# First stage of a hybrid mLSTM and attention layer: who issues the loads of x, and where two small gate copies run

## The chip, the cores and the metric

The kernel runs on one core of one Trainium2 chip. The metric is the device time of one execution in microseconds (us). Three executions of the kernel before gave 3497.74, 3498.3 and 3503.58 us; their median is 3498.3 us. All inputs, outputs and intermediate tensors are in 32-bit floating point.

## The reference, cut to what matters

```python
def encoder_layer(x, ...):                      # two groups of tokens: 2048 and 256, 1024 features
    h = rmsnorm(x, norm1_w)
    p = h @ w_in                                # 1024 -> 2848 columns
    mq, mk, mv, mo, gates, aq, ak, av = split(p)
    m_out = mlstm_mixer(mq, mk, mv, mo, gates, ...)   # 8 heads, both directions, output gate mo
    a_out = attention_mixer(aq, ak, av, ...)          # 8 query heads, 2 key heads, normed q and k, rotary
    x = x + concat([m_out, a_out]) @ w_out
    h = rmsnorm(x, norm2_w)
    a, g = split(dwconv3(h @ w_up))
    return x + (silu(g) * a) @ w_down           # then a final rmsnorm
```

The `gates` are 32 columns per token: input and forget gates of 8 heads in two directions. The forget gates go through a log-sigmoid, and running sums and maxima of the gates over the tokens give the stabiliser m, which every mLSTM chunk uses.

## The kernel before, in words

The 2304 tokens are cut into 18 tiles of 128. The work has four stages: the first stage (`phase_a`, with `gate_math` behind it), attention and mLSTM woven into each other, the output projection, and the feed-forward part. Each engine runs its instructions in the order of its own list. A scheduler puts those lists together from the order in which the program emits its operations and from its own estimate of their times, so an edit in one place can shift neighbours in another. A helper, `issue_after`, lets the program say that some instruction comes behind a given one in that list.

The first stage goes through the tiles in a fixed order, tiles 16 and 17 first and then 0 to 15. In this document "tile n" is the n-th in that order, from 0 to 17. For each tile:

- `front_a` (L167) loads x (512 KB), squares it on ScalarE (ACT, L173), and adds the eight pieces in three steps on GpSimd (POOL, L179 and L180). `rstd_bc` sums over the features with a small matmul (L127), adds epsilon on VectorE (DVE, L130), raises to the power -1/2 on POOL (L131), and spreads the result with another small matmul (L133).
- `front_b` (L183) multiplies x with it on DVE (L187), makes a rounded copy on ACT (L188) and the rest on DVE (L189), and stores both, 1 MB, to `n_d` from the queue of SyncE (SP, L190). Once DVE is through, the buffer of x is free. There are three such buffers beside the two that tiles 0 and 1 use.
- `mm` (L222) does the 48 matmuls of the tile for attention's columns and the gates (L232).
- `post_a` and `post_b` evict on ACT (L241, L243), sum squares (DVE, L251), raise to the power on POOL (L96, L97), apply norm and rotary on DVE (L257 to L275, with one rounding on ACT, L274), and store q to `q_d` from the SP queue (L276).
- `post2` transposes k on PE (L310), evicts on ACT (L311) and stores it from the ACT queue.
- `gates` (L279) works on groups of two or four tiles: log-sigmoid on DVE and ACT, then for each tile a copy that spreads the gates over 64 columns (`gp`, L299, DVE), two transposes on PE (L303), and an eviction of 40 x 256 elements into `rows` (L304, DVE).

The loop interleaves these: while tile n is multiplied, `front_b` of tile n+3 and `front_a` of tile n+4 run. The load of x is inside `front_a`, so it is emitted four tiles ahead, and it is issued from the SP queue, which also carries the stores to `n_d` and `q_d` and the loads of the mLSTM weights (L103).

Once the last tile is multiplied, `gate_math` scans `rows` (L372, L374), makes the stabiliser and its derived tables, and stores `nm_d` (L454); PE meanwhile begins the mLSTM projections (L688, L698), whose PSUM buffer is single.

In the mLSTM, `out_a` (L783) prepares a chunk: a load of m (`dm`, from `nm_d`, L785) and, for every second chunk of the first three head pairs, a load of the output gate (`ogr`, from `og_d`, L797), both issued from the POOL queue. The loads of attention's keys and values (L489 to L492) are issued from POOL too.

Of the kernel before, what the change touches and what calls it, by code (L numbers as in the profile page):

```python
# [9 lines left out]
F32 = mybir.dt.float32  # L10
F32R = mybir.dt.float32r
AF = mybir.ActivationFunctionType
# [5 lines left out]
P = 128  # L18
D = 1024
NCC = D // P  # L20
T1, T2 = 2048, 256
T = T1 + T2
NT = T // P
# [18 lines left out]
NX0 = 2  # L42
# [42 lines left out]
def f32(ap):  # L85
    return ap.bitcast(F32)
# [50 lines left out]
def phase_a(g, tc, sw, st_x, after_x, after_mm, after_pj, wm):  # L137


    nc = g.nc  # L140
    with ExitStack() as st:
# [9 lines left out]
        sx = st_x.enter_context(tc.tile_pool(name="a_x", bufs=2, side="right", reuse_waits="tile"))  # L151
# [8 lines left out]
        order = list(range(NT1, NT)) + list(range(NT1))  # L160

        first = [sw.tile([P, D], F32, tag="w", name=f"first{k}", bufs=WB) for k in range(8)]
        xw = [first[k].rearrange("p (c t) -> p c t", c=NCC) for k in range(NX0)]

        xs = {}

        def front_a(i):  # L167

            n = order.index(i)
            x = xw[n] if n < NX0 else sx.tile([P, NCC, P], F32, tag="x", name=f"x{i}", bufs=3)  # L170
            nc.sync.dma_start(x, g.xT[i])
            xq = sx.tile([P, NCC, P], F32, tag="xq", name=f"xq{i}", bufs=2)
            nc.scalar.activation(xq, x, AF.Square, scale=1.0 / 32.0)  # L173
            sq = sf.tile([P, P], F32, tag="sq", name=f"sq{i}")
            if n == 0:
                nc.vector.tensor_reduce(sq, xq.rearrange("p c t -> p t c"), AX.X, ALU.add)
            else:
                for k in (4, 2):
                    nc.gpsimd.tensor_tensor(xq[:, 0:k], xq[:, 0:k], xq[:, k:2 * k], ALU.add)  # L179
                nc.gpsimd.tensor_tensor(sq, xq[:, 0], xq[:, 1], ALU.add)  # L180
            xs[i] = x, rstd_bc(g, sf, pp if n else pj_, [sq], P, "rs" if n else "pj", f"a{i}", bufs=2)
# [11 lines left out]
        def weights(cs):  # L193
            for c in cs:
                r = first[NX0 + c] if NX0 + c < 8 else sx.tile([P, D], F32, tag="x", name=f"ra{c}", bufs=3)
                split(g, ws[c][:, 0, :], ws[c][:, 1, :], g.w_a[c], r[:, 0:800], g.n1w[:, c:c + 1])

        def tables():
            nc.sync.dma_start(bgb, g.b_gates.to_broadcast([P, 32]))
            for n in (slice(0, 4), slice(4, NT1)):  # L200
                nc.sync.dma_start(tab[:, n, 0], g.rope.rearrange("(n p) a d -> p n a d", p=P)[:, n])
            nc.sync.dma_start(qkw[:, 0, :], g.q_norm_w.to_broadcast([P, HD]))
            nc.sync.dma_start(qkw[:, 1, :], g.k_norm_w.to_broadcast([P, HD]))
            for t in gps:
                nc.gpsimd.memset(t, 0.0)
            for a in range(2):
                for r in range(2):
                    for h in range(2):
                        o, s = r * 32 + h * 16, r * 32 + (1 - h) * 16
                        nc.vector.tensor_copy(rot[:, a, o:o + 16], qkw[:, a, s:s + 16])  # L210
            for t in (qkw, rot):
                nc.vector.tensor_scalar(t[:, 0, :], t[:, 0, :], 0.125, None, ALU.mult)


        def tables2(n):
            eng = nc.gpsimd if n.start else nc.vector
            for a in (1, 0):
                for r, t in enumerate((qkw, rot)):
                    eng.tensor_tensor(tab[:, n, a, r, :], tab[:, n, 0, r, :],
                                            t[:, a:a + 1, :].to_broadcast([P, n.stop - n.start, HD]), ALU.mult)  # L220
# [58 lines left out]
        def gates(i0, n):  # L279

            f = g.gtm[:, i0:i0 + n, 1, :]
            t4 = sp.tile([P, 4, 4, 16], F32, tag="t4", name=f"t4_{i0}", bufs=1)
            na, u, ln, dl = (t4[:, k, 0:n] for k in range(4))
            nc.vector.scalar_tensor_tensor(na, f, -1.0, f, ALU.mult, ALU.min)
            nc.scalar.activation(na, na, AF.Exp)
            yield
            nc.vector.tensor_scalar(u, na, 1.0, None, ALU.add)
            nc.vector.scalar_tensor_tensor(dl, u, 1.0, na, ALU.subtract, ALU.subtract)
            nc.scalar.activation(ln, u, AF.Ln)
            nc.vector.tensor_scalar(u, u, -0.5, 1.5, ALU.mult, ALU.add)  # L290
            nc.vector.tensor_tensor(dl, dl, u, ALU.mult)
            yield
            nc.vector.tensor_tensor(ln, ln, dl, ALU.subtract)
            nc.vector.scalar_tensor_tensor(f, f, 0.0, ln, ALU.min, ALU.subtract)
            for i in range(i0, i0 + n):
                if i % 2 == 0:
                    yield
                gp = gps[i % 3]
                nc.vector.tensor_copy(gp.rearrange("p a (b z) -> p a b z", b=2)[:, :, :, 0:8],  # L299
                                      g.gtm[:, i].rearrange("p a (b h) -> p a b h", b=2))  # L300
                pg = pp.tile([40, 2, P], F32, tag="pk", name=f"pg{i}")
                for a in range(2):
                    nc.tensor.transpose(pg[:, a, :], gp[:, a, 0:40], g.ident)  # L303
                nc.vector.tensor_copy(g.rows[:, :, i * P:(i + 1) * P], pg)  # L304

        def post2(i, kz):
            pk = pp.tile([P, 2, P], F32R, tag="pk", name=f"pk{i}")
# [3 lines left out]
            nc.scalar.activation(kT, f32(pk), AF.Copy)  # L311
            nc.scalar.dma_start(g.k_d[:, :, i * P:(i + 1) * P].rearrange("g p t -> p g t"), f32(kT))

        front_a(order[0])
        front_b(order[0])
        weights(range(0, 3))
        front_a(order[1])
        front_b(order[1])
        weights(range(3, 6))
        front_a(order[2])  # L320
        front_b(order[2])
        weights(range(6, NCC))
        tables()
        tables2(slice(0, 2))
        front_a(order[3])
        prev = None
        steps = []
        for n, i in enumerate(order):
            pj, = mm(i)
            if n:  # L330
                post2(order[n - 1], prev)
            if n == NT - 1:
                st_f.close()
                after_mm()
            qk, r = post_a(i, pj)
            with ExitStack() as behind:
                if n + 3 < NT:
                    behind.enter_context(tc.issue_after(front_b(order[n + 3]).ins))
                    if n + 4 == NT:
                        st_x.close()  # L340
                        after_x()
                prev = post_b(i, qk, r)
                if steps:
                    for _ in range(2 if n == NT - 1 else 1):
                        next(steps[0], None)
                if n < 7:
                    tables2(slice(2 * n + 2, min(2 * n + 4, NT1)))
                if wm:
                    wm.pop(0)()
            if n + 4 < NT:  # L350
                front_a(order[n + 4])
            if n == NT - 1:
                st_j.close()
                after_pj()
            if n % 4 == 1:
                for _ in (steps.pop() if steps else ()):
                    pass
                steps = [gates(*((NT1, 2) if n == 1 else (i - 3, 4)))]
                next(steps[0])
# [284 lines left out]
def mlstm(g, tc, s1, sp, sw, sn, pj_, pm):  # L644


    nc = g.nc
# [133 lines left out]
    def out_a(s, i):  # L781
        nm = f"{s.p}_{i}"
        o = Pair()  # L783
        o.dm = sp.tile([P, 2, 2, P], F32, tag="dm", name="dm" + nm, bufs=DMB)
        nc.gpsimd.dma_start(o.dm.rearrange("p d h l -> p (d h l)"),  # L785
                          g.nm_d[i, 4 * s.p:4 * s.p + 4].rearrange("r l -> (r l)").unsqueeze(0).to_broadcast([P, 4 * P]))
        for d in range(2):
            sgn = 1 - 2 * d
            nc.gpsimd.affine_select(out=o.dm[:, d], in_=o.dm[:, d], compare_op=ALU.is_ge, fill=NEG, base=0,
                                    pattern=[[0, 2], [sgn, P]], channel_multiplier=-sgn)  # L790
            for h in range(2):
                nc.scalar.activation(o.dm[:, d, h], o.dm[:, d, h], AF.Exp,
                                     bias=tm[:, i, 0, d, 2 * s.p + h:2 * s.p + h + 1])
        if s.p < LASTP:
            if i % 2 == 0:
                s.og = s1.tile([P, 2, P], F32, tag="ogT", name="ogr" + nm, bufs=OTB)
                nc.gpsimd.dma_start(s.og, g.og_d[s.p, i // 2])  # L797
            o.og = s.og[:, i % 2]
        return o

# [87 lines left out]
    s = weights(0)  # L888
    yield from proj_steps(s)
    for p in range(4):  # L890
# [3 lines left out]
        if p < 3:  # L894
# [4 lines left out]
            while True:  # L899
                a, b = next(outs, None), next(ps, None)  # L900
# [3 lines left out]
            s = s2  # L904
# [558 lines left out]
```

## Time and profile before

| what | value |
|---|---|
| median of the runs | 3498.3 us (3497.74 to 3503.58) |
| the profiled execution, its own time | 3496.09 us |
| its span in the trace | 3494.4 us |
| TensorE (PE) busy | 3401.6 us |
| VectorE (DVE) busy | 2346.9 us |
| ScalarE (ACT) busy | 1680.2 us |
| GpSimd (POOL) busy | 1101.4 us |
| HBM read and written | 315.55 MB and 82.72 MB |

PE is busy nearly all the time, so the places to read are its idle stretches, what ended each of them, and the granted clock, which is the share of full speed at which PE may run. In a list of instructions each row has the start and the duration in us, the engine, the line of the kernel, the operation, what it writes and reads, and in brackets how long the engine sat idle before and what released it. "SPq" and "POOLq" are the queues of those engines. In a list of waits each row names who waited, for whom, the total in us, how often, and the longest. The first stage lasts from the start to about 212 us, the gates' tail behind it to about 250 us.

### The profile page before, as it was taken

The page shows a single profiled execution, that of the slowest core. Times are in us where ns is not written, and L with a number is a line of the kernel's source. Part 1 is how long each engine was busy: PE and PEld are TensorE (multiplying, and loading weights), DVE is VectorE, ACT ScalarE, POOL GpSimd, SP SyncE. Part 2 cuts the span into 40 slices and gives each one's busy share as a digit, 9 for nine tenths or more (in the row PEclk, how much of TensorE's full clock was granted, in tenths as well). Part 3 has the DMA queues.
Part 4 walks back from the last instruction along what each step waited for, and adds up shares of the span by engine and source line. Part 5 has one row for each costly group of instructions (what it writes and reads, how often), then busy time and mean ns, then how long its engine had stood idle before and what let it go on. Part 6 is the DMA issues. An engine that isn't in the chain of part 4 may idle for free. (4 is left out here: it accounts for less than half of the span.)

```text
span 3494.4 us, 53250 instructions
## 1 busy us (share of the span) xinstructions
PE 3401.6 (97%) x19538; PEld 3027.3 (87%) x19538; DVE 2346.9 (67%) x4008; ACT 1680.2 (48%) x3809; POOL 1101.4 (32%) x1298
## 2 busy tenths in 40 slices
PE   7999999999999999999999999999999999999998
PEld 6788777777777777767788999998999999999998
DVE  6874364546544555664445888878888878887777
ACT  4544354444444454453333544445544445555555
POOL 6752022213231321311125333225433224422222
PEclk9999999999999999999999999999999999999999
DMA  6764233233243434442247332213423213312221
GB/s 218 244 196 135 81 119 96 83 119 95 89 128 111 136 112 136 130 138 79 86 157 249 120 105 96 73 69 122 143 98 103 73 67 124 140 63 70 73 68 54
DMA packets 252629, 401.76 MB, mean 115 GB/s; under 512 B 27984, under 2 KB 152688, under 8 KB 252368
## 3 DMA queue, kind: packets, MB, share of 16 engines
q1 hardware_dynamic: 220272, 355.87, 30.5%
q0 software_dynamic: 10640, 31.86, 3.1%
q10 hardware_dynamic: 21456, 10.62, 1.0%
q8 instruction: 154, 2.52, 0.3%
q14 instruction: 107, 0.88, 0.1%
HBM read 315.55 MB, written 82.72 MB: 114 GB/s over the span
## 5 line engine op out<-in xcount | busy, mean ns | idle before, releaser
L1203 PE MATMUL pd<-act,wd 128*128 128x384 f32 (+1 forms) x3120 | 591.2, 335 | 17.0 <-DVE acc L1205 11.3
L1203 PEld LDWEIGHTS pd<-act,wd 128*128 128x128 f32 x3120 | 539.5, 188 | 24.0 <-DVE acc L1205 14.7
L581 PE MATMUL pv<-pe,vv 128*128 128x512 f32 x1040 | 514.5, 593 | 0.2
L547 DVE TENSOR_REDUCE mx<-px 128x1 f32<-128x512 f32 (+1 forms) x528 | 342.5, 673 | 194.2 <-PE px L546 192.5
L1065 PE MATMUL pa<-nt,wut 128*128 128x386 f32 (+2 forms) x2376 | 455.0, 339 | 1.5 <-ACT u L1081 1.5
L1065 PEld LDWEIGHTS pa<-nt,wut 128*128 128x128 f32 x2376 | 422.2, 190 | 1.8 <-ACT u L1081 1.8
L571 ACT ACTIVATE pe<-ps 128x512 f32<-128x512 f32 x520 | 292.5, 595 | 262.2 <-PE ps L570 258.6
L1159 DVE SCALAR_TENSOR_TENSOR y<-u,cw,y 128x768 f32<-128x768 f32 (+1 forms) x264 | 307.9, 1167 | 36.0 <-ACT y L1152 29.0
L1070 POOL TENSOR_TENSOR tw<-ru 128x512 f32<-128x512 f32 x66 | 96.4, 1461 | 744.5 <-DMA ru<-w_up 536.5
L1205 DVE TENSOR_TENSOR acc<-pd,acc 128x384 f32<-128x384 f32 (+1 forms) x544 | 281.4, 538 | 37.5 <-PE pd L1203 36.5
L1081 ACT ACTIVATE u<-pa 128x386 f32<-128x386 f32 (+2 forms) x264 | 128.8, 488 | 327.1 <-PE pa L1065 325.0
L581 PEld LDWEIGHTS pv<-pe,vv 128*128 128x128 f32 x1040 | 189.0, 189 | 82.5 <-issue 57.8
L569 PE MATMUL ps<-qq,kk 128*128 128x512 f32 x520 | 249.8, 483 | 0.1
L949 PE MATMUL po<-cmx,wo 128*128 128x256 f32 x1728 | 241.7, 290 | 1.6 <-DVE wo L106 1.6
L949 PEld LDWEIGHTS po<-cmx,wo 128*128 128x128 f32 x1728 | 220.8, 190 | 25.4 <-issue 17.8
L546 PE MATMUL px<-kk,qq 128*128 128x512 f32 (+1 forms) x528 | 224.4, 455 | 2.6 <-ACT pe L571 1.7
L688 PE MATMUL mj<-mn,wm 128*128 128x256 f32 x1296 | 212.2, 303 | 5.8 <-ACT og L702 4.5
L688 PEld LDWEIGHTS mj<-mn,wm 128*128 128x128 f32 x1296 | 180.7, 193 | 34.7 <-issue 20.6
L570 PE MATMUL ps<-qm,kl 65*128 65x512 f32 x520 | 207.4, 402 | 0.0
L698 PE MATMUL mv<-wm,mn 128*128 128x256 f32 x1296 | 206.3, 298 | 0.9 <-ACT qb L694 0.9
L698 PEld LDWEIGHTS mv<-wm,mn 128*128 128x128 f32 x1296 | 178.4, 192 | 22.3 <-issue 14.2
L232 PE MATMUL pj<-w_a,n1T 128*128 128x512 f32 (+1 forms) x864 | 178.9, 362 | 5.7 <-ACT n1T L188 4.5
(283 smaller groups left out, 6629.8 us busy)
## 6 DMA issues: line engine op xcount, KB each, us to landing
ru<-w_up SPq DMA_DIRECT2D x132, 512.0 KB, 3.2
mn<-n_d SPq DMA_DIRECT2D x216, 256.0 KB, 3.3
rd<-w_down SPq DMA_DIRECT2D x66, 512.0 KB, 3.3
n_d<-n1T SPq DMA_DIRECT2D x18, 1024.0 KB, 5.6
dm<-nm_d POOLq DMA_DIRECT2D x72, 256.0 KB, 3.6
mjn<-n_d SPq DMA_DIRECT2D x72, 256.0 KB, 3.0
mvn<-n_d SPq DMA_DIRECT2D x72, 256.0 KB, 3.2
q_d<-qz SPq DMA_DIRECT2D x18, 512.0 KB, 3.1
```

The costliest lines, as they stand in the source:

```text
L546: nc.tensor.matmul(ps[:, 0:w], s.qq[:, t * P:(t + 1) * P], s.kv[z0][0][:, 0:w], start=True, stop=True)
L547: nc.vector.tensor_reduce(s.mx[:, t, z0:z0 + 1], ps[:, 0:w], AX.X, ALU.max)
L569: nc.tensor.matmul(ps[:, 0:N], kk[:, kc:kc + P], s.qq[:, 0:N], start=True, stop=False)
L571: nc.scalar.activation(pe[:, z, 0:N], ps[:, 0:N], AF.Exp)
L581: nc.tensor.matmul(s.pv[:, 0:N], s.kv[kp // 2][2][:, kt % 4, :], pe[:, z, 0:N], start=(kt == 0), stop=(kt == s.nk - 1))
L688: nc.tensor.matmul(pj[:, o], s.w[c][:, a, o * P:(o + 1) * P], nT[c][:, :, h, :], start=(c + o + k == 0), stop=(c == NCC - 1 and k == 2 and ...
L698: nc.tensor.matmul(pv[:, o], nT[c][:, o, a, :], s.w[c][:, h, 256:512], start=(c + o + k == 0), stop=(c == NCC - 1 and k == 2 and o == 1))
L949: nc.tensor.matmul(po[:, o], wo[c][z // 2][:, a, n], mx[c][:, h, :], start=(c == 0 and k == 0), stop=(c == NCC - 1 and k == 2))
L1065: nc.tensor.matmul(p, w[:, aa, c, :], ops[k][:, c, bb, 0:n], start=c == 0 and i == 0 and not add, stop=c == NCC // 2 - 1 and i == 2, skip_ ...
L1159: nc.vector.scalar_tensor_tensor(y[:, s:e], u[:, s + k:e + k], cw[:, k, jj:jj + 1], y[:, s:e], ALU.mult, ALU.add)
L1203: nc.tensor.matmul(po, wds[j][c // 4][:, aa, c % 4 * P:(c % 4 + 1) * P], acts[j][:, bb, z0:z1], start=(j == 0 and k == 0), stop=(j == len( ...
L1205: nc.vector.tensor_tensor(accs[c][:, z0:z1], po, accs[c][:, z0:z1], ALU.add)
```

## The change

The load of x leaves `front_a` and becomes `load_x`. The first four tiles' loads still go out from SP; the other 14 go out from POOL. In the loop they are emitted for tile n+5, just ahead of `front_a` of tile n+4. The number of buffers stays three. The copy `gp` goes from DVE to POOL, the eviction into `rows` from DVE to ACT. The load of the output gate must stand behind the chunk's load of m in POOL's list. Nothing else in the program text changes.

```diff
+        def load_x(i):
+            n = order.index(i)
+            xs[i] = x = xw[n] if n < NX0 else sx.tile([P, NCC, P], F32, tag="x", name=f"x{i}", bufs=3)
+            (nc.sync if n < 4 else nc.gpsimd).dma_start(x, g.xT[i])
+
         def front_a(i):
 
             n = order.index(i)
-            x = xw[n] if n < NX0 else sx.tile([P, NCC, P], F32, tag="x", name=f"x{i}", bufs=3)
-            nc.sync.dma_start(x, g.xT[i])
+            x = xs[i]
...
-                nc.vector.tensor_copy(gp.rearrange("p a (b z) -> p a b z", b=2)[:, :, :, 0:8],
+                nc.gpsimd.tensor_copy(gp.rearrange("p a (b z) -> p a b z", b=2)[:, :, :, 0:8],
                                       g.gtm[:, i].rearrange("p a (b h) -> p a b h", b=2))
...
-                nc.vector.tensor_copy(g.rows[:, :, i * P:(i + 1) * P], pg)
+                nc.scalar.activation(g.rows[:, :, i * P:(i + 1) * P], pg, AF.Copy)
...
+        load_x(order[0])
         front_a(order[0])
         front_b(order[0])
         weights(range(0, 3))
+        load_x(order[1])
...
+        load_x(order[3])
         tables()
         tables2(slice(0, 2))
+        load_x(order[4])
         front_a(order[3])
...
+            if n + 5 < NT:
+                load_x(order[n + 5])
             if n + 4 < NT:
                 front_a(order[n + 4])
...
-        nc.gpsimd.dma_start(o.dm.rearrange("p d h l -> p (d h l)"),
+        ins = nc.gpsimd.dma_start(o.dm.rearrange("p d h l -> p (d h l)"),
                           g.nm_d[i, 4 * s.p:4 * s.p + 4].rearrange("r l -> (r l)").unsqueeze(0).to_broadcast([P, 4 * P]))
...
-                nc.gpsimd.dma_start(s.og, g.og_d[s.p, i // 2])
+                with tc.issue_after(ins.ins):
+                    nc.gpsimd.dma_start(s.og, g.og_d[s.p, i // 2])
```

More of the change, by code (lines that the diff above doesn't have):

```diff
@@ L319, in phase_a @@
         weights(range(3, 6))
+        load_x(order[2])
         front_a(order[2])
```

## The prediction

> **What bounds the kernel now.** I read the page's first part, then the busy times by stretch, then the waits of the first stage, then single rows of the timeline. First the span and the engines' shares:
>
> ```profile
> span 3494.4 us, 53250 instructions
> PE 3401.6 (97%) x19538; PEld 3027.3 (87%) x19538; DVE 2346.9 (67%) x4008; ACT 1680.2 (48%) x3809; POOL 1101.4 (32%) x1298
> ```
>
> PE is idle for 3494.4 - 3401.6 = 92.8 us in all. The stretches (length, busy us of PE, PEld, DVE, ACT, POOL, granted clock, DMA) show where:
>
> ```profile
> 13.30:54.00 40.70, 34.44 (x166) 28.50 (x167) 22.36 (x38) 15.67 (x21) 33.52 (x49) 0.98 0.55 181
> 54.00:212.00 158.00, 148.99 (x818) 128.75 (x817) 138.46 (x272) 78.07 (x121) 98.62 (x80) 0.96 0.70 234
> 212.00:250.00 38.00, 31.36 (x235) 29.70 (x236) 28.10 (x61) 12.73 (x26) 19.16 (x49) 0.91 0.52 165
> ...
> 400.00:500.00 100.00, 100.00 (x564) 78.61 (x562) 56.70 (x131) 47.91 (x132) 20.87 (x44) 1.00 0.36 113
> ...
> 1280.00:1840.00 560.00, 552.46 (x3190) 436.80 (x3189) 300.33 (x641) 241.83 (x606) 118.95 (x183) 1.00 0.39 120
> ```
>
> The first stage is bound by PE with DVE close behind: from 54 to 212 us PE is busy 149.0 of 158 us and DVE 138.5. What the change can win there is PE's idle time, 40.7 - 34.4 = 6.3 us, 158 - 149.0 = 9.0 us and 38 - 31.4 = 6.6 us, and the time lost to a lower clock, (1 - 0.98) x 40.7 = 0.8, (1 - 0.96) x 158 = 6.3 and (1 - 0.91) x 38 = 3.4 us. That is 21.9 + 10.5 = **32.4 us**, the most that any edit in this stage can give. From 400 to 500 us PE has no gap, so what is won ahead of it is kept, and nothing more is won by handing work over earlier.
>
> Who ends PE's gaps, from 54 to 212 us and then from 212 to 250 us, with two waits of other engines from the first of these windows:
>
> ```profile
> PE rs_a L127 <- POOL sq L180: 6.9, 3, 3.3
> PE rs_a L127 <- DVE x L187: 1.1, 1, 1.1
> ...
> PE pk L310 <- DVE qz L275: 3.0, 2, 1.6
> PE mj L688 <- ACT og L702: 2.2, 1, 2.2
> PE pg L303 <- DVE rows L304: 0.9, 1, 0.9
> ...
> ACT xq L173 <- DMA x<-xT: 15.4, 6, 6.3
> DVE qz L275 <- ACT qz L274: 6.9, 7, 2.1
> ```
>
> PE never waits for a load here. It waits for the sums of squares on POOL (6.9 of the 9.0 us), and in the tail for DVE's q and ACT's evictions. ACT does wait for x, 15.4 us, but ACT is busy half the time; its wait counts only where something else stands behind it.
>
> **The change part by part: the loads of x.** Five tiles ahead is less than it sounds. There are three buffers, so the load of tile n+5 needs the one that `front_b` of tile n+2 sets free. The load of tile 9 shows how near to that point the present order already is:
>
> ```profile
> 84.72 1.21 DVE L189 TENSOR_TENSOR n1T<-x,n1T 128x1024 fp32r<-128x1024 f32 x1
> 85.97 0.52 SPq L190 DMA_DIRECT2D n_d<-n1T  x1
> 86.54 0.66 SPq L171 DMA_DIRECT2D x<-xT  x1
> 93.95 1.06 ACT L173 ACTIVATE xq<-x 128x1024 f32<-128x1024 f32 x1 [6.32 <-DMA x<-xT]
> 96.29 0.82 DVE L275 TENSOR_TENSOR qz<-t,qz 128x640 fp32r<-128x640 f32 x1 [2.10 <-ACT qz L274]
> 106.65 0.38 PE L127 MATMUL rs_a<-ones,sq 128*128 128x2 f32 x2 [3.29 <-POOL sq L180]
> ```
>
> DVE is through with tile 6 at 84.72 + 1.21 = 85.93, and the load goes out at 86.54: only 0.6 us are to be had by an earlier issue. But the load sits behind the 1 MB store in one queue, and its data are there only at 93.9, 7.4 us later. What the kinds of transfer take from issue to landing (KB each, median us):
>
> ```profile
> x<-xT SPq DMA_DIRECT2D x16, 512.0 KB, 7.1
> n_d<-n1T SPq DMA_DIRECT2D x18, 1024.0 KB, 5.6
> ru<-w_up SPq DMA_DIRECT2D x132, 512.0 KB, 3.2
> dm<-nm_d POOLq DMA_DIRECT2D x72, 256.0 KB, 3.6
> ```
>
> The same 512 KB land in 3.2 us where no such store is ahead. POOL's queue is another one, so the load would share the DMA engines with the store instead of following it. No row shows 512 KB from POOL; the bounds are 3.2 us (alone) and 7.1 us (as now). I take 4.5, nearer to the POOL row with its 3.6. Then tile 9's x is there at 86.0 + 4.5 = 90.5, 3.3 us earlier. ACT's square has the rounding for q behind it, and DVE waited 2.10 us for that. So DVE's chain gains 2.1 us, which is what the sum that PE waits for at 106.65 hangs on (POOL's last add of tile 10 stands behind a power that needs DVE's sum). The gap of 3.29 shrinks to 1.2. A stretch of half clock follows this gap; the windows put 6.3 us of loss on such stretches between 54 and 212 us, and I count 0.9 for the chance that this one goes. Term: **-3.0 us** (bounds: 0, if the landing stays 7 us, to -3.3 - 1.7).
>
> The Trainium skill's page "DMA: Bandwidth & Descriptors" (section "Issuing engine by pattern") speaks against this edit: transfers from SyncE or ScalarE are said to be generally faster than those from GpSimd, and the section on latency gives about 0.6 against 1 us to the first byte. By that alone each load would land 0.4 us later, an estimate from those two figures, and the term above would be +0.4 instead of -3.0; the rows here say that the place in the queue, some 3 to 4 us, is the larger thing.
>
> Each issue costs POOL time, which SP had in plenty. The only POOL loads with many rows:
>
> ```profile
> L785 POOL DMA_DIRECT2D dm<-nm_d x72: 536/607/649, 270.2 to 1500.5; - x72
> ```
>
> 14 issues by 0.61 us are 8.5 us. POOL is busy 98.6 of 158 us, so 59 us are free, and I count nothing. If the gaps don't fit, the cost falls on sums and powers (second rival).
>
> One load gets later. In the built order of the changed program the load of tile 5 stands on POOL behind the adds of tiles 3 and 4, where SP now sends it at 39.78:
>
> ```profile
> 39.78 0.66 SPq L171 DMA_DIRECT2D x<-xT  x1
> ...
> 42.41 0.87 POOL L180 TENSOR_TENSOR sq<-xq 128x128 f32<-128x128 f32 x2
> 47.18 1.28 POOL L179 TENSOR_TENSOR xq<-xq 128x512 f32<-128x512 f32 x1 [3.89 <-ACT xq L173]
> 48.42 1.07 POOL L131 TENSOR_TENSOR rcol_a<-rcol_a,mhalf 128x1 f32<-128x1 f32 x2
> 49.02 1.01 PE L133 MATMUL rs_a<-ident,rcol_a 128*128 128x128 f32 x4 [0.80 <-POOL rcol_a L131]
> ```
>
> POOL is through with those adds at 42.4, so the load goes out there, 2.6 us later, and at 4.5 us lands at 46.9 + 0.6 for the issue = 47.5; now POOL's add of tile 5 begins at 47.18 after 1.1 us of squaring, so it moves to 48.6. The powers of tiles 3 and 4 stand behind this add, and PE waits for them at 49.02. Term: **+1.4 us** (bounds: -1 if it lands in 3.2 us and the sum tightens elsewhere, +4 if it lands in 7.1).
>
> **The gates' copies.** The three operations concerned, with durations least/median/greatest in ns:
>
> ```profile
> L299 DVE COPY gp<-gtm x18: 161/174/1268, 92.7 to 224.5; 128x32 f32<-128x32 f32 x18
> L304 DVE COPY rows<-pg x18: 352/408/417, 104.8 to 228.8; 40x256 f32<-40x256 f32 x18
> L311 ACT ACTIVATE kT<-pk x18: 361/384/390, 70.4 to 241.2; 128x256 fp32r<-128x256 f32 x18
> ```
>
> DVE loses 18 x (0.174 + 0.408) = 10.5 us. Counted along DVE's list, 13 of the first and 10 of the second stand between 54 and 212 us (6.3 us), 5 and 8 behind (4.1 us). ACT gains 18 evictions of the form of L311, 18 x 0.38 = 6.9 us, on an engine with 158 - 78 = 80 us to spare. POOL's copy has no row; it lies between 0.17 us (DVE's) and 0.6 us (a POOL DMA issue), so 3 to 11 us, again in POOL's 59 us. The hidden price is the order: an eviction on ACT that stands behind a rounding of q waits for DVE as well, and PE's next transpose waits for its PSUM buffer. PE's waits of this kind are now 0.9 us; I leave it so, with bounds 0 and 5.
>
> Of the other gaps from 54 to 212 us, 9.0 - 3.3 = 5.7 us, 4.7 hang on DVE's pace (the sums at 139 and 151 us and the wait on L187). DVE has 6.3 of 138.5 us less to do; I take half of the 4.7: **-2.4 us** (bounds 0 and -4.7).
>
> **The tail.** PE's gaps of 6.6 us are q on DVE (3.0), the output gate on ACT (2.2) and rows (0.9). Two rows carry it:
>
> ```profile
> 229.98 0.74 ACT L274 ACTIVATE qz<-t 128x640 fp32r<-128x640 f32 x1 [6.12 <-DVE t L272]
> 236.72 0.80 POOL L797 DMA_DIRECT2D ogr<-og_d  x1 [11.09 <-DMA og_d<-og]
> ```
>
> ACT stands 6.12 us at the last tile's q and evicts PE's projection only afterwards. With 4.1 us less on DVE, and in the built order this q behind those evictions, the 2.2 us should go, and part of the 3.0. Term: half of 6.1, **-3.0 us** (bounds +2, if the six evictions into rows hold PE's buffers, to -6.6 - 3.4). The POOL row is the third edit: POOL stands 11.09 us at the output gate's load, with attention's keys behind it. PE waits for no key in this stretch, so this I count at nothing; were it not for the projections that fill PE, it would be worth up to those 11 us.
>
> **Later.** In the built program PE's list agrees again with the old one from about 430 to 1280 us, but for one swap, and from 1840 us on; between these the scheduler shuffles it. PE is idle 560 - 552.5 = 7.5 us there, so a shuffle is worth -3 to +5 us; I take 0.
>
> Sum: -3.0 + 1.4 - 2.4 - 3.0 = **-7.0 us**. The profiled execution took 3496.1 us and would take 3489.1; against the median of 3498.3, which is 2.2 above it, **3491**.
>
> **The rivals.**
>
> First, the stalls go for good. If loads that land in 4.5 us and a lighter DVE remove most of what PE waits for from 54 us on, the gain is 9.0 + 6.6 us of gaps, less 1.4 at tile 5, and the clock's loss of some 3: about -17, **3481**. For it: 6.9 of 9.0 us have one cause, POOL's sums. Against it: those sums hang on DVE, which stays at 132 of 158 us.
>
> Second, and slower: POOL becomes the place where the stage waits. POOL runs in order, and a load that needs a buffer stands until DVE frees it, with sums and powers behind it; the built order has such a load right ahead of the adds of tiles 10, 13 and 15, and two in a row behind the power of tile 5. Price: 0.8 us (issue and hand-over) at each of the four places where PE already waits for POOL, 3.2; at tile 5 2.6 instead of 1.4; two more stretches of half clock at 1.7 each, 3.4: +9, **3507**. It decides if POOL's sums come over 1 us later than now where PE stands; that PE waits 6.9 us for them already speaks for it, POOL's 59 free us against.
>
> Third, nothing that counts: ACT's waits for x shrink, but PE's gaps are set by DVE and the order, and the scheduler's new order takes back what is won: 0, **3498**.
>
> **How the numbers follow.** My forecast, -2 to -12 us, has 0.46, the first rival 0.16, the second 0.22, the third 0.16. About 0.2% (7 us, 3491.3 and 3505.3) is what a measurement of this kernel can tell from no change. The forecast lies on that edge and gives 0.24 to faster and 0.22 to the same; the first rival is faster, the third the same, and of the second 0.18 is slower and 0.04 the same. Faster 0.40, same 0.42, slower 0.18. The range runs from 3479, below the first rival, to 3508, just past the second: it leaves out the outer ends of both, some 0.15. The forecast's own range is 3486 to 3496.
>
> **What would show it.** Right: x lands in 4 to 5 us from POOL, ACT's wait for x falls from 15.4 to under 7 us, the gap at 106.65 is under 2 us, PE's idle time from 54 us to the last tile's matmul is under 6 us, and the mLSTM's first projections stand less than 1 us for ACT. Wrong: POOL rows of L170 with long waits ahead of sums, PE's wait for POOL's sums above 7 us, ACT evictions of rows with PE behind them, or a difference of more than 3 us between 1280 and 1840 us.

## The result and the profile after

| | before | after |
|---|---|---|
| median of the runs, us | 3498.3 | 3505.51 |
| lowest and highest, us | 3494.77 to 3508.11 | 3497.77 to 3514.87 |
| ratio after / before, 95% interval | | 1.0022 [1.0013, 1.0031] |
| profiled execution: own time, span, us | 3496.09, 3494.4 | 3501.88, 3500.2 |
| first matmul of the mLSTM projections begins at, us | 214.5 | 219.1 |

The change made the kernel slower by 0.22%, 7.7 us when the ratio is put on 3500 us. The forecast was 3491.

First the page of the changed kernel, span and busy times:

```profile
span 3500.2 us, 53252 instructions
...
PE 3401.6 (97%) x19538; PEld 3025.3 (86%) x19538; DVE 2350.9 (67%) x3972; ACT 1683.3 (48%) x3827; POOL 1110.0 (32%) x1330
```

PE's busy time is the same to 0.1 us, so what these two executions differ by is PE's idle time. DVE runs 36 instructions fewer and is busy no less. The busy times by stretch (length, then PE, PEld, DVE, ACT, POOL, granted clock, DMA) show that PE is idle for longer in each part of the stage:

```profile
13.30:54.00 40.70, 33.42 (x163) 28.03 (x164) 21.68 (x36) 15.65 (x21) 34.21 (x52) 0.98 0.55 180
54.00:212.00 158.00, 146.14 (x796) 124.14 (x796) 139.79 (x251) 81.78 (x133) 106.26 (x106) 0.97 0.69 231
212.00:250.00 38.00, 30.04 (x221) 28.22 (x219) 23.26 (x39) 14.07 (x32) 14.94 (x40) 0.91 0.44 146
1280.00:1840.00 560.00, 553.75 (x3202) 437.86 (x3201) 304.92 (x652) 239.89 (x605) 123.04 (x188) 1.00 0.40 122
```

PE's idle time went from 6.3 to 7.3 us, from 9.0 to 11.9, and from 6.6 to 8.0. The stretch at 1280 us, whose order the scheduler shuffled, is 1.3 us better. PE's waits, from 54 to 212 us and then from 212 to 250 us, with ACT's wait for x from the first:

```profile
PE pk L314 <- DVE qz L279: 4.3, 3, 3.1
PE rs_a L127 <- POOL sq L184: 2.5, 4, 1.3
PE rs_a L127 <- DVE x L191: 2.2, 2, 1.6
PE rs_a L133 <- POOL rcol_a L131: 1.9, 4, 0.8
...
PE gpt L419 <- DVE rows L385: 4.8, 1, 4.8
PE pk L314 <- DVE gtm L250: 2.8, 1, 2.8
...
ACT xq L177 <- DMA x<-xT: 22.9, 8, 5.5
```

The wait for POOL's sums fell from 6.9 to 2.5 us, as was meant, but waits for q on DVE and for POOL's powers took its place, and in the tail PE now stands 4.8 us for the scan of `rows`. PE and DVE there, after, then before:

```profile
239.68 0.56 PE L419 MATMUL gpt<-ident,rows 40*128 40x40 f32 x6 [4.76 <-DVE rows L385]
235.21 4.41 DVE L385 TENSOR_TENSOR_SCAN rows<-rows 8x2048 f32<-8x2048 f32 x1
```

```profile
233.19 7.04 PE L688 MATMUL mj<-mn,wm 128*128 128x256 f32 x44 [2.22 <-ACT og L702]
234.28 4.41 DVE L374 TENSOR_TENSOR_SCAN rows<-rows 8x2048 f32<-8x2048 f32 x1
```

The scan ends only 0.9 us later than before. But in PE's new list the transposes that need it stand ahead of the projection that PE ran meanwhile before.

ACT waits 22.9 us for x instead of 15.4. The view of the line that loads x, first after (L170: durations in ns, first and last start, then issue to landing), then before (L171):

```profile
L170 POOL DMA_DIRECT2D x<-xT x14: 530/642/759, 22.4 to 175.7; - x14
...
DMA to landing us min/median/max: 3.8/7.0/10.3
```

```profile
DMA to landing us min/median/max: 3.6/7.1/9.6
```

The data come no sooner. The load still meets the 1 MB store, from another queue (changed kernel, the load of tile 9):

```profile
88.47 0.53 SPq L194 DMA_DIRECT2D n_d<-n1T  x1
...
88.74 0.64 POOL L170 DMA_DIRECT2D x<-xT  x1 [2.25 <-DVE n1T L193]
```

POOL stood 2.25 us at this load for x's buffer, then issued it 0.27 us behind the store. From the issue of the store (of tile n-3) to the landing of x (of tile n) it is 8.0 us before and 8.1 us after, in the mean of tiles 5 to 17.

### The profile page after: what moved, and what is told of

The parts are those of the page before. It is cut to its first block, busy times and chain, and to the rows that moved or that the text cites. A ratio compares the mean times of both kernels' runs of the same rounds, so it can differ in the third digit from the quotient of the medians.

```text
span 3500.2 us, 53252 instructions
## 1 busy us (share of the span) xinstructions
PE 3401.6 (97%) x19538; PEld 3025.3 (86%) x19538; DVE 2350.9 (67%) x3972; ACT 1683.3 (48%) x3827; POOL 1110.0 (32%) x1330
## 4 chain that ended last, share of the span: by engine, by line
PE 74%; DVE 10%; DMA 6%; issue 4%; POOL 3%; ACT 3%; SPq 0%; POOLq 0%; ACTq 0%; DVEq 0%
PE pa L1077 12%; PE pd L1215 11%; PE pv L592 11%; PE pc L1077 6%; PE po L961 4%; PE mj L699 4%; PE mv L709 4%; PE ps L580 3%; PE ps L581 3%; PE px L557 3%; PE pb L1077 3%; PE mN L836 1%; DVE y L1171 1%; PE mv L725 1%; PE mj L725 1%
## 5 line engine op out<-in xcount | busy, mean ns | idle before, releaser
L961 PEld LDWEIGHTS po<-cmx,wo 128*128 128x128 f32 x1728 | 220.0, 190 | 22.9 <-issue 17.0
L605 DVE RECIPROCAL rs<-rs 64x512 f32<-64x512 f32 x36 | 120.2, 3340 | 129.8 <-ACT rs L601 129.7
```

The costliest lines, as they stand in the source:

```text
L961: nc.tensor.matmul(po[:, o], wo[c][z // 2][:, a, n], mx[c][:, h, :], start=(c == 0 and k == 0), stop=(c == NCC - 1 and k == 2))
```

## The experiments

Theory A: POOL is what costs. The loads take POOL's time and make it stand, with sums and powers behind them. Theory B: the two copies cost it. Theory C: the loss is made behind the first stage, by order or by chance. All results in one table; "us" is the ratio less 1, times 3500. "At 860" is how much later than in the kernel before one matmul of the mLSTM projections begins, in the profiled execution (860.3 us there, the 961st of its line): it shows what the first stage left, roughly: e1 and e7 run the same lists on every engine and still differ by 2.5 us there.

| kernel | median, us | ratio [95%] | us | at 860 |
|---|---|---|---|---|
| the change | 3505.51 | 1.0022 [1.0013, 1.0031] | +7.7 | +4.1 |
| e1 loads only | 3511.18 | 1.0026 [1.0014, 1.0038] | +9.1 | +4.6 |
| e2 both copies only | 3504.36 | 1.0011 [1.0003, 1.0020] | +3.8 | +3.4 |
| e3 output gate only | 3495.76 | 0.9994 [0.9985, 1.0002] | -2.1 | +1.6 |
| e4 loads five ahead, from SP | 3500.63 | 1.0005 [0.9996, 1.0015] | +1.7 | +2.2 |
| e5 load before store | 3498.38 | 0.9996 [0.9988, 1.0005] | -1.4 | -4.4 |
| e6 the change, loads from SP | 3497.40 | 0.9991 [0.9982, 1.0000] | -3.1 | +1.1 |
| e7 POOL loads, four ahead | 3508.16 | 1.0026 [1.0014, 1.0039] | +9.1 | +7.1 |
| e8 rows on ACT only | 3493.74 | 0.9980 [0.9971, 0.9989] | -7.0 | -4.0 |
| e9 gp on POOL only | 3504.96 | 1.0013 [1.0005, 1.0022] | +4.5 | +3.3 |
| e10 loads from ACT | 3497.94 | 0.9997 [0.9988, 1.0005] | -1.0 | -2.4 |
| e11 four loads back on SP | 3512.58 | 1.0036 [1.0024, 1.0048] | +12.6 | +10.0 |
| e12 rows on ACT, output gate | 3492.81 | 0.9979 [0.9969, 0.9988] | -7.3 | -4.2 |
| e13 small loads on POOL | 3504.67 | 1.0014 [1.0006, 1.0023] | +4.9 | +4.3 |
| e14 an eighth of x from POOL | 3510.09 | 1.0030 [1.0017, 1.0042] | +10.5 | +11.7 |
| e15 e12, loads from ACT | 3491.06 | 0.9982 [0.9973, 0.9990] | -6.3 | -5.9 |
| e16 e12, load before store | 3496.07 | 0.9990 [0.9981, 0.9998] | -3.5 | +1.5 |
| e17 one load on POOL | 3501.79 | 1.0009 [0.9997, 1.0020] | +3.1 | -2.4 |
| e18 twelve loads on POOL | 3506.82 | 1.0019 [1.0009, 1.0029] | +6.6 | +5.5 |

The expectations took the size of earlier results from medians or means, so it differs by up to 2 us from this column.

Not all of "us" need be waiting. Each run has a mean granted clock on record; its mean over the runs is 0.9902 in e1, 0.9901 in e2 and 0.9924 in e8, against 0.9911, 0.9911 and 0.9912 for the kernel before, measured beside them. Since 0.001 of 3500 us is 3.5 us, an estimate is that a lower clock makes up 3 of e1's 9.1 us and nearly all of e2's 3.8, and a higher one 4 of e8's 7.0. Whether PE's gaps bring on the stretches of half clock, no run here tells.

### One edit at a time

e1 is the change with the copies and the output gate's load as before; e2 and e3 are the kernel before with

```diff
-                nc.vector.tensor_copy(gp..., g.gtm...)                # e2, and alone in e9
+                nc.gpsimd.tensor_copy(gp..., g.gtm...)
-                nc.vector.tensor_copy(g.rows[...], pg)                # e2, and alone in e8
+                nc.scalar.activation(g.rows[...], pg, AF.Copy)
-                nc.gpsimd.dma_start(s.og, g.og_d[s.p, i // 2])        # e3
+                with tc.issue_after(ins.ins):
+                    nc.gpsimd.dma_start(s.og, g.og_d[s.p, i // 2])
```

> Only the first edit: 14 loads of x from POOL, emitted for tile n+5; both gate copies on DVE and the output gate's load as before. Theory A (the loads cost the time: the 512 KB land no sooner from POOL's queue, 7 us, and later tiles' loads go out behind POOL's other work): 3 to 8 us slower than the kernel before, the first mLSTM projection 3 us or more later, median landing 6.5 us or more. Theory B (the two gate copies cost it, as an eviction on ACT with PE behind it): within 2 us of the kernel before. Theory C (the difference comes behind the first stage, where the order of the lists is shuffled or from one execution to the next): the first mLSTM projection within 1.5 us of before, the end anywhere within 5 us. The prediction's own steps would give -3.0 + 1.4 = -1.6 us here.

> Only the second edit: the copy gp on POOL and the eviction into rows on ACT; loads of x from SP four tiles ahead, output gate's load as before. Theory A (the loads cost the time): -5 to 0 us against the kernel before, since DVE gives up 10.5 us of copies; the tail from 212 to 250 us no longer than before. Theory B (the copies cost it): 3 to 8 us slower, with the loss in the tail or at the places where PE waits for rows or for POOL. Theory C (the loss comes behind the first stage): the first stage within 1.5 us of before. The prediction's own steps would give -2.4 - 3.0 = -5.4 us here.

> Only the third edit: the output gate's load stands behind the chunk's load of m in POOL's list; everything in the first stage as before. Theories A and B: within 2 us of the kernel before, because PE waits for no key in the tail. Theory C (the shuffled order behind the first stage costs the time): 3 to 7 us slower, with the difference arising between 400 and 1840 us and the first stage unchanged to 0.5 us. The prediction gave 0 here with bounds -3 and +5.

The loads alone cost 9.1 us, as much as the whole change (7.7) within the intervals: theory A. The two copies cost 3.8, so B holds for a part. The output gate's edit shuffles PE's list behind the first stage and is worth -2.1 us, with an interval from -5 to +1: C gets nothing from it.

### Who issues the loads

In e4 the loads stand where the change puts them, but all go out from SP; in e10 the 14 go out from ACT; in e7 only the engine is changed:

```diff
-            (nc.sync if n < 4 else nc.gpsimd).dma_start(x, g.xT[i])   # the change, in load_x
+            nc.sync.dma_start(x, g.xT[i])                             # e4; e6 with the other edits kept
+            (nc.sync if n < 4 else nc.scalar).dma_start(x, g.xT[i])   # e10
-            nc.sync.dma_start(x, g.xT[i])                             # before, in front_a
+            (nc.sync if n < 4 else nc.gpsimd).dma_start(x, g.xT[i])   # e7
```

> Loads of x emitted for tile n+5 as in the change, but all 18 issued from SP; copies and output gate's load as before. It parts the queue from the place of emission. If POOL's queue costs the time (the load waits for a buffer with POOL's sums and powers behind it, or is issued behind POOL's work): this one is within 2 us of the kernel before, and the loads-only kernel 3 us or more slower than this one. If the new order of emission costs it: both are equally slow, to 2 us.

> The loads of x as in the change, but the 14 go out from ACT's queue instead of POOL's; copies and output gate as before. If what costs is POOL's own time and order (sums and powers and loads in one list): within 3 us of the kernel before, although the queue is not SP's either. If it is enough that the loads leave SP (their share of the DMA engines, or the order that the scheduler then builds): 7 to 10 us slower, like the loads from POOL.

> The loads of x are emitted for tile n+4, as before, but issued from POOL; nothing else. The built order is that of the loads-only kernel on every engine, so if the place of emission counted, nothing could show it here. Theory A (POOL's queue costs it, in the first stage): same as the loads-only kernel to 2 us, that is +7 to +12 against the kernel before, with the first mLSTM projection 4 us or more late and x issued 2 to 4 us behind the store at tiles 5, 8, 16 and 17. Theory C (the part of the loss behind the first stage, 9 us in the one profile of the loads-only kernel, is chance of one execution): this profile shows less than 5 us of it.

> The whole change, except that all 18 loads of x go out from SP: copies on POOL and ACT, output gate's load behind m. Theory A (POOL's queue is what costs): 4 to 9 us faster than the changed kernel, that is 3497 to 3502 us. Theory B (copies and order cost it): within 2 us of the changed kernel, 3504 to 3508. Adding the single edits measured so far, +1.4 for the emission, +4.4 for the copies and -3.3 for the output gate against the kernel before, would give 3502.

From SP +1.7, from ACT -1.0, from POOL +9.1, twice. Emission four or five tiles ahead gives the same lists on every engine when POOL issues (e7, e1), so "five ahead" did nothing by itself. With the loads on SP, the change is 3.1 us faster than the kernel before, with an interval from -6 to 0. That the loads cost the time if POOL issues them, and not if SP or ACT does, is shown.

By which path they cost it is not. Changing the engine makes the scheduler rebuild the other lists too: in e7 PE's list parts from that of the kernel before at 45 us, ACT's at 68 and DVE's at 74 (times in the kernel before). So there are two candidates, POOL's own time and the rebuilt lists.

In e7 the loss arises from 163 us on: from the first matmul of tile 13 to the first mLSTM projection e7 takes 58.2 us (163.1 to 221.3), the kernel before 50.9 (163.6 to 214.5). POOL in e7, then ACT and DVE:

```profile
160.58 1.96 POOL L97 TENSOR_TENSOR rqk<-rqk,mhalf 128x10 f32<-128x10 f32 x1
162.50 0.62 POOL L171 DMA_DIRECT2D x<-xT  x1
163.15 2.68 POOL L179 TENSOR_TENSOR xq<-xq 128x512 f32<-128x512 f32 x2
...
171.15 3.49 POOL L179 TENSOR_TENSOR xq<-xq 128x512 f32<-128x512 f32 x2
174.60 0.64 POOL L171 DMA_DIRECT2D x<-xT  x1
175.27 0.51 POOL L180 TENSOR_TENSOR sq<-xq 128x128 f32<-128x128 f32 x1
...
181.54 1.06 ACT L173 ACTIVATE xq<-x 128x1024 f32<-128x1024 f32 x1 [1.57 <-DMA x<-xT]
...
183.58 1.47 DVE L189 TENSOR_TENSOR n1T<-x,n1T 128x1024 fp32r<-128x1024 f32 x1 [2.22 <-ACT n1T L188]
```

and the same two loads before, from SP:

```profile
155.59 0.66 SPq L171 DMA_DIRECT2D x<-xT  x1
...
164.06 0.66 SPq L171 DMA_DIRECT2D x<-xT  x1
```

The load stands behind a power at 162.50 and between the adds of one sum at 174.60. The last x arrives 11.1 us later than before. Only 1.8 us of this arise at POOL's issue: it sends the load 2.34 us behind the store, where SP took 0.57. Another 0.6 us are in the landing. The other 8.8 us are there already, since the store goes out at 172.26 instead of 163.49: DVE takes up that tile (L187) 9 us later, in e7, then before:

```profile
168.67 1.21 DVE L187 TENSOR_TENSOR x<-x,rs_a 128x1024 f32<-128x1024 f32 x1
```

```profile
159.66 1.21 DVE L187 TENSOR_TENSOR x<-x,rs_a 128x1024 f32<-128x1024 f32 x1
```

In DVE's rebuilt list the norm and rotary of one more tile stand ahead of it. They do so in e4 too, where the last x comes some 6 us later than before, at a loss of 1.7 us in the runs. So both candidates are at work in e7. ACT stands for x at 181.54 with the rounding of another tile behind, and DVE waits 2.22 us for that rounding. PE's waits from 163 us to the mLSTM in e7, then before:

```profile
PE pk L310 <- DVE qz L275: 5.6, 3, 3.2
PE pk L310 <- DVE rcol_a L130: 1.8, 1, 1.8
PE rs_a L127 <- POOL sq L180: 1.6, 1, 1.6
```

```profile
PE pk L310 <- DVE qz L275: 2.0, 2, 1.6
PE pg L303 <- ACT kT L311: 0.4, 1, 0.4
PE pg L303 <- DVE gp L299: 0.3, 1, 0.3
```

9.0 us against 2.7: the difference, 6.3, is nearly all of the 7.3. Only 1.6 of the 9.0 names POOL; the rest reaches PE through DVE. e1 and e18, with the same lists on DVE and ACT, take 58.2 and 58.3 us for this stretch. The changed kernel takes 52.2 (166.9 to 219.1): it is late before that, 0.3 us at the start of tile 12 and 3.3 at tile 13, with a wait of 3.1 us for q in between. e6, with its loads from SP, has a wait of 3.0 us for q one tile later.

### Is an early x worth anything

In e5 all loads go out from SP, and the store of tile n+2 is held back until the load of tile n+5 is issued; the rest is as in the kernel before.

```diff
             if n + 5 < NT:
-                load_x(order[n + 5])               # and the store inside front_b
+                load_x(order[n + 5])               # from SP
+                with tc.issue_after(xl[n + 5].ins):
+                    store(*late.pop(n + 2))
```

> All loads of x from SP, copies and output gate's load as before; the store of tile n-3 to n_d is held back until the load of tile n is issued, so that the 512 KB go ahead of the 1 MB instead of behind it. Expected landing of x: 3.5 to 4.5 us after its issue, against 7.1, and about 4 us after the buffer is free, against 8. Theory A (an early x is worth what the prediction said, and the change only failed to deliver it): 2 to 6 us faster than the kernel before, the gap of 3.3 us before tile 8's sum under 1.5 us. Theory B (x's landing is hidden, PE waits for something else): within 2 us of the kernel before although x lands 3 us earlier.

```profile
DMA to landing us min/median/max: 3.6/4.1/9.1
```

The landing is what the prediction had hoped for. The profile of e5 is 4.4 us ahead at 860 us and loses it later, by a stall and a stretch of half clock near 1210 us and in the feed-forward part; its runs show -1.4 us [-4, +2]. e10, whose loads leave from ACT at the same moment as the store, has the same kind of landing and -1.0 us:

```profile
L170 ACTq DMA_DIRECT2D x<-xT x14: 334/371/405, 20.2 to 158.0; - x14
...
DMA to landing us min/median/max: 3.6/4.3/9.0
```

So an x that lands 3 us sooner, with the lists that come with it, is worth at most 4 us, likelier 1 to 2.

### What of it costs on POOL

e11 puts the loads of tiles 5, 8, 16 and 17 back on SP, e18 those of tiles 4 and 5, e17 takes only that of tile 4 to POOL. In e13 POOL issues 14 loads of 4 KB that nothing reads; in e14 it loads an eighth of each x.

```diff
+            (nc.sync if n in (0, 1, 2, 3, 5, 8, 16, 17) else nc.gpsimd).dma_start(x, g.xT[i])   # e11, in load_x
+            (nc.sync if n < 6 else nc.gpsimd).dma_start(x, g.xT[i])                             # e18, in front_a
+            (nc.gpsimd if n == 4 else nc.sync).dma_start(x, g.xT[i])                            # e17, in front_a
+                nc.gpsimd.dma_start(tiny, g.xT[i][:, 0, 0:8])                                   # e13, beside SP's load
+                nc.sync.dma_start(x[:, 0:7], g.xT[i][:, 0:7])                                   # e14
+                nc.gpsimd.dma_start(x[:, 7:8], g.xT[i][:, 7:8])
```

> The loads of x as in the change, but those of tiles 5, 8, 16 and 17, which POOL issued 2.3 to 4.4 us behind the store, go out from SP; ten are left on POOL. If the late issue costs the time: at most 2 us slower than the kernel before, and the loss of some 7 us between tile 13 and the first mLSTM projection is gone. If the issue time on POOL costs it (0.64 us each between sums and powers): 5 to 7 us slower, ten fourteenths of what the loads-only kernel lost.

> The kernel before, and beside each of the 14 loads of x that the change takes to POOL, which stay on SP, POOL issues a load of 4 KB into a scratch tile that nothing reads; it need not stand for x's buffer. If the issue time on POOL costs it (14 issues of about 0.6 us in POOL's list): 5 to 10 us slower than the kernel before. If what costs is POOL standing for a buffer: within 3 us of the kernel before.

> The kernel before, with each of the 14 loads of x cut in two: seven eighths from SP, one eighth (64 KB) from POOL, which has to stand for x's buffer as in the change. If issue time is all: like the kernel with small loads on POOL, to 2 us. If standing for the buffer costs it: 4 us or more slower than that one, and 7 to 10 us slower than the kernel before. If the transfer of the whole x through POOL's queue were the cause: within 3 us of the kernel before.

> The kernel before with one load, that of tile 4, issued from POOL; all other lists are those of the kernel before. If this load shifts POOL's string of table products so that DVE is held up in part of the executions: the median 2 to 6 us above the kernel before, the highest runs near 3508 to 3512, and a row of DVE at about 22 us that takes several us where the profile caught it. If the two profiles that showed it were chance or came from other differences: within 1.5 us of the kernel before.

> Loads of x for tiles 6 to 17 from POOL, those of tiles 4 and 5 from SP; DVE's and ACT's lists are those of the loads-only kernel. If the start of the stage carries the loss: within 3 us of the kernel before. If it is POOL's time and order between tiles 12 and 17: 6 to 10 us slower, like all loads on POOL. If both: 3 to 6 us slower, with a smaller spread than the 13 to 17 us of the kernels with all loads on POOL.

e13 was to give the price of the issues alone, and doesn't. The scheduler put all 14 small loads into the first 54 us, and POOL stood 6.3 us for the buffer of the small tile:

```profile
L174 POOL DMA_DIRECT2D tiny<-xT x14: 537/568/744, 1.8 to 53.8; - x14
...
  DMA tiny<-xT: 6.3, 2
```

Tile 11, which begins 85 us after the last small load, is still 0.5 us earlier than before; tile 12 is 4.5 us later. So little of e13's 4.9 us can be the time of its issues; it speaks for the rebuilt lists, which part from those before at 24 us on PE and 23 on DVE.

e18 keeps 6.6 of the 9.1 us and +5.5 at 860, so most of the loss is made in the body of the stage. e11 and e14 don't tell what they were made for: both lost some 8 us by tile 2, when POOL had issued no load but that of tile 4. e11 there, DVE, POOL (first and last of its string of products) and PE, and the same operation of DVE before:

```profile
22.15 7.62 DVE L216 TENSOR_SCALAR rot<-rot 128x64 f32<-128x64 f32 x1
...
22.23 2.96 POOL L223 TENSOR_TENSOR tab<-tab,qkw 128x128 f32<-128x128 f32 x7
...
28.86 1.62 POOL L223 TENSOR_TENSOR tab<-tab,qkw 128x128 f32<-128x128 f32 x3
...
32.45 1.22 PE L236 MATMUL pj<-w_a,n1T 128*128 128x512 f32 x2 [7.17 <-ACT n1T L192]
```

```profile
22.86 0.45 DVE L212 TENSOR_SCALAR rot<-rot 128x64 f32<-128x64 f32 x1
```

DVE's operation ran beside POOL's string for 7.62 us; that the string held it is inferred. In e11 and e14 the load of tile 4 stands on POOL right ahead of that string, but so it does in e1, e7 and e17, whose profiles don't show the hold. Whether some of their executions have it stays open: e17's runs spread from 3493.1 to 3511.5 us with a median 2.2 us above the kernel before, which would fit, but its interval holds 0. e17 is the one kernel with a load on POOL and the lists of PE, DVE and ACT as before. Between issue time, standing for the buffer and the rebuilt lists the loss is not divided.

### The two copies apart, and what to keep

> Only the eviction into rows goes from DVE to ACT; gp stays on DVE, loads and output gate as before. The kernel with both copies moved was 4.4 us slower. If the eviction is its cause (an ACT eviction behind a rounding of q): 3 to 5 us slower here. If gp on POOL or the order of DVE's list is (its profile shows DVE 2.8 us idle for the load of mhw, with the last q behind it): within 2 us of the kernel before, unless DVE's list has mhw early here too. The prediction gave the eviction 0, with bounds 0 and 5.

> Only the copy gp goes from DVE to POOL; the eviction into rows stays on DVE, loads and output gate as before. Both copies moved were 4.4 us slower, the eviction alone 5.6 us faster than the kernel before. If the two add up, gp on POOL costs 8 to 12 us. If the loss with both comes from their coming together (DVE's list then has mhw ahead of the last q), gp alone is within 3 us of the kernel before. The prediction gave POOL's copy nothing (3 to 11 us of POOL's time, in its 59 free us).

> The two edits that gained by themselves: the eviction into rows on ACT (-5.6 us) and the output gate's load behind m (-3.3 us); gp on DVE, loads of x from SP as before. If they add up: 7 to 11 us faster than the kernel before, 3489 to 3493 us. If the output gate's gain was chance of those runs, or hangs on an order that the other edit changes: 4 to 6 us faster.

The eviction on ACT gains 7.0 us, gp on POOL loses 4.5. Together they make +3.8, not -2.5: one kernel's lists are not the sum of two others'. In e2 DVE stands for a small load (`mhw`) with the last q but one behind it, which neither e8 nor e9 has:

```profile
215.67 0.27 DVE L650 TENSOR_SCALAR mhw<-mhw 128x4 f32<-128x4 f32 x1 [2.82 <-DMA mhw<-mhw]
215.78 0.83 DVE L275 TENSOR_TENSOR qz<-t,qz 128x640 fp32r<-128x640 f32 x1
```

In e9 the price is in the tail, where the gp copies stand behind POOL's other work (PE's wait from 212 to 250 us):

```profile
PE pg L303 <- POOL gp L299: 2.5, 2, 2.3
```

e12 leaves POOL out and is 7.3 us faster than the kernel before. Two more tries add a sooner x to it, without POOL: loads from ACT (e15) and load before store (e16).

> The change with POOL relieved of its two new duties: the 14 loads of x from ACT's queue, gp back on DVE; rows on ACT and output gate's load behind m as in the change. If the edits add up: -6.9 (rows and output gate) - 1.7 (loads from ACT), 8 to 9 us faster than the kernel before, about 3491. If ACT with loads and evictions becomes the place of the wait: at most 5 us faster.

> Eviction into rows on ACT, output gate's load behind m, and the loads of x from SP ahead of the store that frees their buffer's neighbour; gp on DVE. If the edits add up: -6.9 - 1.3, about 8 us faster than the kernel before, 3491 to 3492. If the earlier x is hidden behind the other two: 6 to 7 us faster, as without it.

e15 has the lowest median, 3491.06 us, but by the intervals e12 and e15 can't be told apart; e16 is slower than both by its median. The sooner x adds nothing that can be measured. The change's aim, less waiting, is reached by taking work from DVE to ACT and none to POOL: in e12 PE's idle time falls from 6.6 to 3.0 us between 212 and 250 us, and from 9.0 to 8.3 between 54 and 212.

## Why the prediction was wrong

- **What bounds the stage.** Right as far as it goes: PE's gaps in the first 250 us grew, and the changed kernel is 4.1 us late at 860 us. It wins 2.9 us of this back by the start of the feed-forward part (before: 1894.7 us), as e3 wins 2.4, and falls back by 4.6 us in that part. There every other profile here, of faster kernels too, falls back by 0.5 to 9.1 us against that of the kernel before, whose execution, 3496.09 us, lies below its median. So one pair of profiles does not tell where the 7.7 us of the runs arise.
- **Loads of x, -3.0 us.** Wrong, in both of its halves. The landing was taken as 4.5 us, since the load would no longer sit behind the store in one queue; it measured 7.0. The gap that stood at 106.65 us did shrink from 3.29 to 1.32 us, as worked out:

```profile
108.50 0.38 PE L127 MATMUL rs_a<-ones,sq 128*128 128x2 f32 x2 [1.32 <-POOL sq L184]
```

  But it begins where PE had already come 3.1 us late to tile 7, so nothing was won: tile 8 begins 0.2 us later than before. The stretch of half clock behind the gap is gone, but a new one as long (3.4 us) stands at 86.6. And where x did land in 4.1 us (e5), the runs gained 1.4 us, with an interval from -4 to +2.
- **Fourteen issues on POOL, counted at nothing.** This is the step that failed most: "POOL is busy 98.6 of 158 us, so 59 us are free", and so the loads were to gain 1.6 us. On POOL they measured +9.1, against +1.7 for the same emission from SP. POOL's free time is waiting time of a chain from ACT to DVE and POOL and back (in the kernel before, from 54 to 212 us, 40.7 us for DVE and 16.3 for ACT), and the rows of e7 show loads inside that chain, with sums behind them. But they also show DVE's rebuilt list, which the prediction left out as well; how the 9.1 us divide between the two stays open.
- **Tile 5's load later, +1.4.** Right: PE's wait at that place went from 0.80 to 2.3 us, and tile 3 begins 1.8 us later.
- **The copies, -2.4, and the tail, -3.0.** Wrong in sum: +3.8 us (e2). Right for the eviction, -7.0 us, more than both terms. Wrong for gp on POOL, again counted at nothing, +4.5 us. With both moved, PE's list in the tail has it stand for the scan, 4.8 us in the changed kernel and 3.7 in e2. e8 and e9 have no such wait, but e13, which moves neither copy, has 4.4: it comes with the rebuilt lists.
- **The output gate's load, 0, and the later order, 0.** Right within the interval (-2.1 us).
- **The rivals.** The second, in which POOL becomes the place where the stage waits, has the right sign and the nearest number, 3507 against 3505.51. Its point of decision, POOL's sums over 1 us later where PE stands, was not how it showed: PE's wait for sums fell, and the delay reached PE through q and the rounding on DVE and ACT. It had 0.22, because the mean share of POOL's time spoke against it. That its number came so close is partly luck, since its sum has no term for DVE's later turn.

By parts the prediction had -1.6 for the loads and -5.4 for the copies and the tail; they measured +9.1 and +3.8. With the output gate's -2.1 the parts add up to +10.8, the change measured +7.7, within what such sums hold here.

## What to carry to other kernels

An engine's free time in the page is no proof of room for new work if the engine is a link of the chain that feeds the bound: here 14 issues of 0.64 us, 9.0 us in all, were counted at nothing and cost 9.1, part of it, by e7's rows and e13, through the lists of other engines that the scheduler rebuilt. So compare those lists too, before and after. A load on POOL's queue did not pass a larger store that was issued 0.3 us ahead of it; issue the load first. Before two copies are moved together, move each alone, and look at where the small loads land in the rebuilt lists.

## What the runs showed of the hardware

A load of 512 KB beside a 1 MB store: issued from SP 0.4 us ahead of the store it lands in 4.1 us (e5, median), from ACT at the same time in 4.3 (e10), from POOL 0.3 us behind it in 7.0, from SP 0.6 us behind it in 7.1. Loads from POOL that went out 4.4 and 3.5 us behind the store (tiles 5 and 16 of the changed kernel) landed in 3.8 and 4.0 us, so POOL's queue is not slow by itself; that of tile 8, 3.4 us behind, took 8.3. Why 0.3 us make that difference between ACT and POOL, no run here tells.

The Trainium skill's page "DMA: Bandwidth & Descriptors" (section "Queues, rings and completion order") says that a DMA engine takes turns between the queues that have work for it, packet by packet; by that the load would be in when about as much of the store is. The loads from ACT, at 4.3 us, agree, those from POOL, at 7.0 us, do not.

A DVE operation on 64 elements per partition took 7.62 us (e11) and 5.42 us (e14) beside POOL's string of products, against 0.45 before. The Trainium skill's page "SBUF — State Buffer" (section "Who interferes with whom") describes a port pair that DVE and GpSimd share as a lock held for one whole instruction. The two long rows fit that one blocks the other, but they last over a dozen of POOL's products, each of some 0.4 us. In the kernel before, the same operation ran beside the same string in its 0.45 us, so that the string is the cause is not shown.
